# Eight instead of nine seven-product pairs in the first half of the down projection, and a later last up group

## The chip, the cores and the metric

The kernel runs on one core of a Trainium2 chip. The core has a matmul engine (PE, with its weight loads shown apart as PEld), a vector engine (DVE), a scalar engine (ACT), GpSimd (POOL) and SyncE (SP); here POOL and SP mainly issue transfers (DMAs). Each engine works through its own queue in order and waits for the others by semaphores. The metric is the device time of one execution in microseconds (us).

## The reference

One layer of a decoder: 256 tokens of width 2048, all in float32. The part that matters here is the gated MLP with a causal convolution of width 3:

```python
h = rms_norm(x, ffn_norm_g[i])
u = h @ w_up[i]                      # 2048 -> 2 x 5632
a, g = jnp.split(u, 2, axis=-1)
a = causal_dwconv(a, conv_w[i], conv_b[i])
x = x + (jax.nn.gelu(a, approximate=False) * g) @ w_down[i]   # 5632 -> 2048
gate = jax.nn.sigmoid(rms_norm(x, ple_norm_g[i]) @ w_ple_gate[i])
x = x + gate * (p[i].astype(x.dtype) @ w_ple_proj[i])
```

Before it stand the token mixers (an mLSTM and a forgetting attention) with their projections `w_in` and `w_out`.

## The kernel before, in words

**Precision.** Each float32 operand is split into a rounded part `hi` and a rest `lo`; a product is three matmuls (`hi*hi`, `hi*lo`, `lo*hi`), which accumulate in one bank of PSUM. In the down projection they stand in `product` at L1017, L1018 and L1019. The function `part` makes the split of a weight block: ACT casts `hi` (L969), then DVE subtracts to get `lo` (L970). Weights come raw from memory, 512 KB a block, by DMAs that SP issues (L955).

**Blocks and buffers.** From the up projection on, all work is a list of blocks (`Unit`), which `run_units` goes through. Blocks are split up to six ahead of the one that the matmuls are at: six sets of `hi` and `lo` (two of them under the name `w`). Raw blocks lie in six slots from the start of the down projection (three `raw`, two `w2raw`, one that shares the tag `pT`), and in three more, the two halves of `EZ` and a part of `Y`, once the last up group has no more use for these. `late["free"]`, set from `LAST_UP`, says from which block on a load may take those three.

**The order.** The Python code gives an order of importance and the dependencies. A planner then sets each engine's queue at compile time by estimated times. So a matmul of a later block may stand ahead of one of an earlier block if the plan expects that one's operands to be late; matmuls into one bank keep their order.

**The up projection.** Eleven groups of 16 blocks. After a group, ACT moves its four banks to `EZ` (`up_rows`, L869), DVE transposes into `Y` (L193), 16 small DMAs issued by POOL move the result back to `EZ` (L199), and then six steps (`up_act`) finish it: `first`, an ACT copy (L881); four convolution steps, each one ACT instruction (L886) and two of DVE (L889); and `last`, an ACT GELU (L895), a DVE multiplication (L896), an ACT cast (L137) and a DVE subtraction (L138). These steps are hooked behind the matmuls of the following blocks. Those of the last group (number 10) fall into the down projection: behind its blocks 5, 6, 6, 7, 8 and 9 (`LAST_UP`). They yield K tiles 40 to 43, which the last two pairs use.

**The down projection.** 44 K tiles of 128, taken as 22 pairs, once for the columns 0 to 1023 (the first half, `down(0, ...)`) and once for 1024 to 2047 (the second half). A plain pair is two blocks (`eight`) of four products each: 2 x 4 x 3 = 24 matmuls. A pair of the list `SEVEN` uses a scheme in the manner of Strassen and Winograd: seven products for eight, so 21 matmuls, in four blocks (`fn1` to `fn4`) of one, two, two and two products. For that it needs sums of the left side, made during the up projection and kept in device memory (`left_sums`, `sums`), which SP loads (L1048, 512 KB into one of two places `S`), and combinations of the raw weights, four DVE subtractions (L1065, L1066, L1075, L1076). Its two raw slots come free only after the fourth split. In both halves nine pairs are in seven products. The second half takes the pairs in the order 0, 1, 2, ..., 21, so that plain pairs and pairs in seven products alternate; the first half has an order of its own, `FIRST`, which begins with the plain pairs 0, 1, 3, 5 (eight blocks), then the pairs 2, 7, 4, 6, 9, 8, 11, 10, ... with 2, 4, 6, 8, 10 in seven products.

**After it.** `sums_done` and `add_rest` add the banks into `xs`; the gate and the last projection follow.

Of the kernel before, what the change touches and what calls it, by code (L numbers as in the profile page):

```python
# [16 lines left out]
S = 256  # L17
# [7 lines left out]
KF = FF // P  # L25
# [9 lines left out]
PARTS2 = 2  # L35

SEVEN = (2, 4, 6, 8, 10, 12, 14, 16, 18)
FIRST = (0, 1, 3, 5, 2, 7, 4, 6, 9, 8, 11, 10, 13, 12, 15, 14, 17, 16, 19, 18, 20, 21)
AHEAD_DMA, AHEAD_SPLIT = 3, 3
PAD = 16  # L40


LO_SHIFT = 16
FRONT = 12
LAST_UP = 9


@with_exitstack
def layer_kernel(
# [19 lines left out]
    def bank(tag, name):  # L69
        return ps.tile([P, 512], F32, tag=tag, name=name)  # L70
# [161 lines left out]
    done = [0]  # L232
# [58 lines left out]
    def wsrc(w, k0, kb, c0, n):  # L291
        return w[0, k0 * P : (k0 + kb) * P, c0 : c0 + n].rearrange("(k p) n -> p k n", p=P)
# [524 lines left out]
    with tc.tile_pool(name="ffn", bufs=1) as fp:  # L817
# [7 lines left out]
        def uT(k, n=1):  # L825

            u, k0 = ((uA, 0), (uB, KD), (uC, KD + 8))[(k >= KD) + (k >= KD + 8)]
            return u[:, k - k0 : k - k0 + n, :]
# [75 lines left out]
        late = {}  # L904
# [70 lines left out]
        def run_units(us, first_late, gate):  # L975
            loaded = split = 0
            for i, u in enumerate(us):
                if i == first_late:
                    v = apool.tile([P, 6, BLK], F32R, tag="aTa", name="w2", bufs=2)
                    room.update(late=2, pT=1, e0=1, e1=1, ring=1)  # L980
                    late.update(gate=gate, free=i + LAST_UP + 1, hi=v[:, 0:2], lo=v[:, 2:4],
                                S=v[:, 4:6].rearrange("p b (i c) -> p b i c", c=256))
# [12 lines left out]
                        break  # L995
                u.fn(*u.parts)

        def down(c0, X_tag, P_tag, sums_done, done, at, pairs):

            banks, seen, us = {}, {}, []
            plain = [p_ for p_ in pairs if p_ not in SEVEN]
            last7 = [p_ for p_ in pairs if p_ in SEVEN][-1]
            total = {"P1": len(SEVEN), "P5": len(SEVEN), "P6": len(SEVEN), "P7": len(SEVEN)}
            for t in range(NT):
                for n in range(2):
                    total[t, n] = 2 * len(plain) + (len(SEVEN) if (t, n) != (1, 1) else 0)

            def product(key, ah, al, hi, lo):  # L1010
                if key not in banks:
                    banks[key] = bank(P_tag if isinstance(key, str) else X_tag, f"dn{key}")
                    seen[key] = 0
                o = banks[key]
                first, last = seen[key] == 0, seen[key] == total[key] - 1
                seen[key] += 1
                pe.matmul(o, ah, hi, start=first, stop=False)  # L1017
                pe.matmul(o, ah, lo, start=False, stop=False)  # L1018
                pe.matmul(o, al, hi, start=False, stop=last)  # L1019

            def left(k, t):
                a = uT(k)[:, 0]
                return a[:, t * P : (t + 1) * P], a[:, 256 + t * P : 256 + (t + 1) * P]

            def half(v, n):
                return v[:, n * 512 : (n + 1) * 512]

            def eight(k, hook):
                def fn(hi, lo):
                    hi, lo = hi[:, 0], lo[:, 0]  # L1030
                    for t in range(NT):
                        for n in range(2):
                            product((t, n), *left(k, t), half(hi, n), half(lo, n))
                    if hook is not None:
                        hook(banks)
                return Unit([wsrc(w_down, k, 1, c0, 1024)], fn)

            def seven(p_, hook):
                k = 2 * p_
                st = {}  # L1040

                def S(i):
                    v = st["S"][:, i - 1]
                    return v[:, 0:P], v[:, P:256]

                def split1(hi, lo):
                    v = late["S"][:, SEVEN.index(p_) % 2]
                    nc.sync.dma_start(out=f32(v).rearrange("p i c -> p (i c)"), in_=sums[SEVEN.index(p_)])  # L1048
                    st["S"] = v
                    part(hi[:, 0:512], lo[:, 0:512], first.raws[0][:, 0:512])  # L1050

                def fn1(hi, lo):
                    product("P1", *left(k, 0), half(hi, 0), half(lo, 0))

                def split2(hi, lo):
                    part(hi, lo, first.raws[1])

                def fn2(hi, lo):
                    product((0, 0), *left(k + 1, 0), half(hi, 0), half(lo, 0))
                    product((0, 1), *S(4), half(hi, 1), half(lo, 1))  # L1060


                def split3(hi, lo):
                    ra, rb_ = first.raws
                    dve.tensor_sub(half(ra, 0), half(ra, 1), half(ra, 0))  # L1065
                    dve.tensor_sub(half(ra, 1), half(rb_, 1), half(ra, 1))  # L1066
                    part(hi, lo, ra)

                def fn3(hi, lo):
                    product("P5", *S(1), half(hi, 0), half(lo, 0))  # L1070
                    product("P7", *S(3), half(hi, 1), half(lo, 1))

                def split4(hi, lo):
                    ra, rb_ = first.raws
                    dve.tensor_sub(half(rb_, 1), half(rb_, 1), half(ra, 0))  # L1075
                    dve.tensor_sub(half(rb_, 0), half(rb_, 0), half(rb_, 1))  # L1076
                    part(hi, lo, rb_)

                def fn4(hi, lo):
                    product((1, 0), *left(k + 1, 1), half(hi, 0), half(lo, 0))  # L1080
                    product("P6", *S(2), half(hi, 1), half(lo, 1))
                    if hook is not None:
                        hook(banks)

                first = Unit([wsrc(w_down, k + i, 1, c0, 1024) for i in range(2)], fn1, split1, 0)
                first.srcs = [v.rearrange("p k n -> p (k n)").unsqueeze(1) for v in first.srcs]
                return [first, Unit([], fn2, split2, 0), Unit([], fn3, split3, 0), Unit([], fn4, split4, 2)]

            for p_ in pairs:
                if p_ in SEVEN:  # L1090
                    us.extend(seven(p_, sums_done if p_ == last7 else None))
                else:
                    for k in (2 * p_, 2 * p_ + 1):
                        us.append(eight(k, done if k == KF - 1 else at.get(k)))
            return us
# [9 lines left out]
        def sums_done(c0):  # L1105

            def f(b):
                both = xs[:, 1, c0 : c0 + 1024].rearrange("p (n c) -> p n c", n=2)
                x00, x01 = (xs[:, 0, c0 + n * 512 : c0 + (n + 1) * 512] for n in range(2))
                right = xs[:, :, c0 + 512 : c0 + 1024]  # L1110

                def twice(v):
                    return v.unsqueeze(1).broadcast_to([P, 2, 512])

                a = ring[:, 2]
                act.copy(a, b["P1"])
                dve.tensor_add(x00, b["P1"], x00)
                dve.tensor_add(a, b["P6"], a)
                dve.tensor_add(right, twice(b["P5"]), right)
                dve.tensor_add(both, twice(b["P7"]), both)  # L1120
                dve.tensor_add(x01, x01, a)
                dve.tensor_add(both, both, twice(a))
            return f

        def add_rest(c0):
            def f(b):
                for n in range(2):
                    for t in range(NT):
                        xc = xs[:, t, c0 + n * 512 : c0 + (n + 1) * 512]
                        dve.tensor_add(xc, b[t, n], xc)  # L1130
                    sumsq(ssq3, c0 // 512 + n, 512)
            return f
# [16 lines left out]
        def x3_columns(*ks):  # L1149
            return lambda *_: [column(x3s[k // 4], k % 4, get_x3T()[:, k], g_ple[:, k : k + 1]) for k in ks]  # L1150
# [116 lines left out]
        us = []  # L1267
        for q in range(KF // 4):
            us += up_group(q)
        first_late = len(us)  # L1270
        us += down(0, "aux", "mm", sums_done(0), add_rest(0), {}, FIRST)
        us += down(1024, "mm", "aux", sums_done(1024), add_rest(1024),
                   {23: x3_squares(0), 27: x3_squares(1),
                    31: x3_columns(0, 1, 2, 3), 35: x3_columns(4, 5, 6, 7)}, range(KF // 2))
        for c0, n in ((0, 512), (512, 512), (1024, 512), (1536, 512)):
            g_ = (units(token_group(w_ple_gate, all_k, get_x3T, c0, n, gate_done(c0, n), tag="aux"))
                  if c0 < D - n else last_group(c0, n))
            p_ = units(token_group(w_ple_proj, [0], lambda: pT["t"], c0, n, proj_done, tag="mm"))
# [7 lines left out]
            at = len(g_) // 2  # L1286
            us += g_[:at] + p_ + g_[at:]
        for q in range(KF // 4):
            for i, job in enumerate(up_act(q)):
                at = (8, 9, 10, 11, 12, 13) if q < KF // 4 - 1 else (5, 6, 6, 7, 8, LAST_UP)  # L1290
                with_after(us[KD * (q + 1) + at[i]], job)
        run_units(us, first_late, gate_at)

# [29 lines left out]
```

## Time and profile before

| what | value |
|---|---|
| median of three runs | 1254.69 us (1253.94 to 1255.78) |
| the profiled execution | 1255.1 us, span 1253.4 us |
| PE busy | 1243.8 us, 99% of the span, 5887 matmuls |
| DVE busy | 832.2 us, 66% |
| ACT busy | 684.9 us, 55% |
| POOL busy | 210.4 us, 17% |
| DMA traffic | 271.27 MB, 216 GB/s in the mean |

The span runs from the first to the last instruction of the program; the execution's own time has 1.7 us more around it. A busy PE is not PE at its fastest: the shown duration of a matmul (389 ns) overlaps with that of the next, so the pace is read from the distance between starts, and a granted clock below 1.00 shows as busy time too. In rows by engine the number before the bracket is busy time, and a bracket tells how long the engine was idle before the instruction and who ended it. A row `x3` has merged three instructions.

### The profile page before, as it was taken

To read this page: it belongs to the slowest core of one execution; us is meant where nothing else is said; L and a number is where in the kernel's file an instruction comes from. 1 tells how busy PE (TensorE), PEld (TensorE's weight loads), DVE (VectorE), ACT (ScalarE), POOL (GpSimd) and SP (SyncE) were. 2 spreads that over 40 slices of the span, in tenths; PEclk is the share of its full clock that TensorE was granted. 3 is DMA by queue.
4 is the path that set the end of the run, shared out by engine and by line. 5 is a ranking of instruction groups with operands and counts; after the bars stand their busy time and mean duration, and the time that the engine had idled before them with its cause. 6 is when DMAs were issued, how large, how long until landed. Compare 5 with 4: busy or idle time off the path is not lost.

```text
span 1253.4 us, 16510 instructions
## 1 busy us (share of the span) xinstructions
PE 1243.8 (99%) x5887; PEld 1051.4 (84%) x5887; DVE 832.2 (66%) x1055; ACT 684.9 (55%) x964; POOL 210.4 (17%) x395
## 2 busy tenths in 40 slices
PE   9999999999999999999999999999999999999998
PEld 7899988888888888888888888888886888888887
DVE  6455568754565655665676576667669998899553
ACT  7655555545554544655565566556546555556542
POOL 2003034100214202112202220221120000050000
PEclk9999999999999999999999999999999999999999
DMA  8667766656667767778877877887897886787560
GB/s 257 177 191 198 216 201 200 191 163 171 201 185 219 218 187 211 211 221 243 235 221 217 247 232 221 224 249 211 243 270 252 291 299 201 258 259 234 172 224 34
DMA packets 133476, 271.27 MB, mean 216 GB/s; under 512 B 14007, under 2 KB 28977, under 8 KB 133393
## 3 DMA queue, kind: packets, MB, share of 16 engines
q1 hardware_dynamic: 119936, 246.51, 65.7%
q0 software_dynamic: 13072, 23.53, 6.6%
q8 instruction: 46, 0.75, 0.2%
q14 instruction: 37, 0.30, 0.1%
q10 hardware_dynamic: 385, 0.16, 0.0%
HBM read 246.54 MB, written 6.83 MB: 202 GB/s over the span
## 4 chain that ended last, share of the span: by engine, by line
PE 95%; DMA 2%; DVE 1%; ACT 1%; issue 1%; POOL 0%; SPq 0%; DVEq 0%; ACTq 0%
PE up L1257 13%; PE up L1258 13%; PE up L1256 13%; PE tg L314 10%; PE tg L313 10%; PE tg L315 10%; PE wg L345 5%; PE wg L346 2%; DMA EZ<-Y 1%; PE dnP L1018 1%; PE dnP L1019 1%; PE dnP L1017 1%; PE dn(1, 0)_8870 L1018 1%; PE dn(0, 1)_8866 L1018 1%; PE dn(0, 1)_8866 L1017 1%; PE dn(0, 0)_8862 L1018 1%
## 5 line engine op out<-in xcount | busy, mean ns | idle before, releaser
L970 DVE TENSOR_TENSOR lo<-raw,hi 128x1024 fp32r<-128x1024 f32 (+1 forms) x219 | 264.4, 1209 | 181.9 <-ACT hi L969 181.6
L969 ACT CAST hi<-raw 128x1024 fp32r<-128x1024 f32 (+1 forms) x219 | 227.3, 1041 | 236.7 <-DMA raw<-in_w_up_dram 126.9
L284 DVE TENSOR_TENSOR lo<-raw,hi 128x1024 fp32r<-128x1024 f32 (+2 forms) x161 | 178.4, 1112 | 149.2 <-ACT hi L282 142.7
L282 ACT CAST hi<-raw 128x1024 fp32r<-128x1024 f32 (+2 forms) x161 | 153.7, 960 | 149.4 <-PE tg L315 81.6
L1258 PE MATMUL up<-hi,x2T 128*128 128x512 f32 x528 | 205.5, 389 | 0.0
L1257 PE MATMUL up<-lo,x2T 128*128 128x512 f32 x528 | 205.4, 389 | 0.0
L1256 PE MATMUL up<-hi,x2T 128*128 128x512 f32 x528 | 204.8, 389 | 0.0
L199 POOL DMA_DIRECT2D EZ<-Y x176 | 93.1, 536 | 175.8 <-DVE Y L193 143.1
L1256 PEld LDWEIGHTS up<-hi,x2T 128*128 128x128 f32 x528 | 99.1, 188 | 20.6
L1258 PEld LDWEIGHTS up<-hi,x2T 128*128 128x128 f32 x528 | 99.1, 188 | 20.5
L1257 PEld LDWEIGHTS up<-lo,x2T 128*128 128x128 f32 x528 | 99.1, 188 | 20.5
L314 PE MATMUL tg<-lo,hT 128*128 128x512 f32 (+1 forms) x288 | 102.9, 357 | 0.0
L313 PE MATMUL tg<-hi,hT 128*128 128x512 f32 (+1 forms) x288 | 101.8, 358 | 0.0
L315 PE MATMUL tg<-hi,hT 128*128 128x512 f32 (+1 forms) x288 | 101.7, 354 | 0.0
L1257 PE MATMUL up<-lo,x2Tb 128*128 128x512 f32 x176 | 68.5, 389 | 0.0
L1258 PE MATMUL up<-hi,x2Tb 128*128 128x512 f32 x176 | 68.5, 389 | 0.0
L345 PE MATMUL wg<-hT,hi 128*128 128x512 f32 x192 | 67.6, 399 | 0.0
L1256 PE MATMUL up<-hi,x2Tb 128*128 128x512 f32 x176 | 65.2, 389 | 0.0
L314 PEld LDWEIGHTS tg<-lo,hT 128*128 128x128 f32 x288 | 54.1, 188 | 5.5
L315 PEld LDWEIGHTS tg<-hi,hT 128*128 128x128 f32 x288 | 54.1, 188 | 5.5
L313 PEld LDWEIGHTS tg<-hi,hT 128*128 128x128 f32 x288 | 53.7, 188 | 5.4
L346 PE MATMUL wg<-hT,lo 128*128 128x256 f32 x192 | 52.1, 284 | 0.0
(762 smaller groups left out, 2428.1 us busy)
## 6 DMA issues: line engine op xcount, KB each, us to landing
raw<-in_w_up_dram SPq DMA_DIRECT2D x176, 512.0 KB, 4.9
raw<-in_w_in_dram SPq DMA_DIRECT2D x79, 512.0 KB, 4.1
raw<-in_w_down_dram SPq DMA_DIRECT2D x43, 512.0 KB, 6.0
raw<-in_w_in_dram SPq DMA_DIRECT2D x48, 344.0 KB, 3.6
raw<-in_w_out_dram SPq DMA_DIRECT2D x32, 512.0 KB, 4.5
EZ<-Y POOLq DMA_DIRECT2D x176, 64.0 KB, 5.6
w2raw<-in_w_down_dram SPq DMA_DIRECT2D x19, 512.0 KB, 5.7
w<-sums SPq DMA_DIRECT2D x18, 512.0 KB, 4.4
```

The source lines that it names most:

```text
L199: pool.dma_start(out=c[32 * b : 32 * b + 32, a::4], in_=y[32 * a : 32 * a + 32, :, b])
L282: act.copy(hi, raw[:, :w])
L284: dve.tensor_sub(lo, raw[:, :w], f32(hi))
L313: pe.matmul(o, ah, hi[:, i, :], start=first, stop=False)
L314: pe.matmul(o, ah, lo[:, i, :], start=False, stop=False)
L315: pe.matmul(o, al, hi[:, i, :], start=False, stop=last)
L345: pe.matmul(o, h[:, i, cols], a, start=first, stop=False)
L969: act.copy(hi, raw)
L970: dve.tensor_sub(lo, raw, f32(hi))
L1256: pe.matmul(o, ah, hi[:, n], start=k == 0, stop=False)
L1257: pe.matmul(o, ah, lo[:, n], start=False, stop=False)
L1258: pe.matmul(o, al, hi[:, n], start=False, stop=k == KD - 1)
```

## The change

Four edits go together. In the first half, pair 2 is computed as a plain pair, so eight pairs are left in seven products (`SEVEN[1:]`); `down` gets this list as an argument. The order `FIRST` becomes 0, 1, 2, 3, 5, then 4, 7, 6, 9, 8, 11, 10, ...: ten plain blocks come first, and then pairs in seven products and plain ones alternate. The place `S` is chosen by a pair's number in the half's own list. And the steps of the last up group are hooked behind blocks 6, 7, 8, 9, 10 and 11 instead of 5, 6, 6, 7, 8 and 9, with `LAST_UP` 11, which moves `late["free"]` by two blocks as well. The second half's list and order stay; the left sums of pair 2 are still made and kept, as the second half uses them.

```diff
 SEVEN = (2, 4, 6, 8, 10, 12, 14, 16, 18)
-FIRST = (0, 1, 3, 5, 2, 7, 4, 6, 9, 8, 11, 10, 13, 12, 15, 14, 17, 16, 19, 18, 20, 21)
+FIRST = (0, 1, 2, 3, 5, 4, 7, 6, 9, 8, 11, 10, 13, 12, 15, 14, 17, 16, 19, 18, 20, 21)
...
-LAST_UP = 9
+LAST_UP = 11
...
-        def down(c0, X_tag, P_tag, sums_done, done, at, pairs):
+        def down(c0, X_tag, P_tag, sums_done, done, at, pairs, sevens):
...
-            plain = [p_ for p_ in pairs if p_ not in SEVEN]
-            last7 = [p_ for p_ in pairs if p_ in SEVEN][-1]
-            total = {"P1": len(SEVEN), "P5": len(SEVEN), "P6": len(SEVEN), "P7": len(SEVEN)}
+            plain = [p_ for p_ in pairs if p_ not in sevens]
+            last7 = [p_ for p_ in pairs if p_ in sevens][-1]
+            total = dict.fromkeys(("P1", "P5", "P6", "P7"), len(sevens))
...
-                    v = late["S"][:, SEVEN.index(p_) % 2]
+                    v = late["S"][:, sevens.index(p_) % 2]
                     nc.sync.dma_start(out=f32(v).rearrange("p i c -> p (i c)"), in_=sums[SEVEN.index(p_)])
...
-        us += down(0, "aux", "mm", sums_done(0), add_rest(0), {}, FIRST)
+        us += down(0, "aux", "mm", sums_done(0), add_rest(0), {}, FIRST, SEVEN[1:])
...
-                    31: x3_columns(0, 1, 2, 3), 35: x3_columns(4, 5, 6, 7)}, range(KF // 2))
+                    31: x3_columns(0, 1, 2, 3), 35: x3_columns(4, 5, 6, 7)}, range(KF // 2), SEVEN)
...
-                at = (8, 9, 10, 11, 12, 13) if q < KF // 4 - 1 else (5, 6, 6, 7, 8, LAST_UP)
+                at = (8, 9, 10, 11, 12, 13) if q < KF // 4 - 1 else (6, 7, 8, 9, 10, LAST_UP)
```

More of the change, by code (lines that the diff above doesn't have):

```diff
@@ L996, in run_units @@
                 u.fn(*u.parts)
-        def down(c0, X_tag, P_tag, sums_done, done, at, pairs):
+        def down(c0, X_tag, P_tag, sums_done, done, at, pairs, sevens):
             banks, seen, us = {}, {}, []
-            plain = [p_ for p_ in pairs if p_ not in SEVEN]
-            last7 = [p_ for p_ in pairs if p_ in SEVEN][-1]
-            total = {"P1": len(SEVEN), "P5": len(SEVEN), "P6": len(SEVEN), "P7": len(SEVEN)}
+            plain = [p_ for p_ in pairs if p_ not in sevens]
+            last7 = [p_ for p_ in pairs if p_ in sevens][-1]
+            total = dict.fromkeys(("P1", "P5", "P6", "P7"), len(sevens))
             for t in range(NT):
                 for n in range(2):
-                    total[t, n] = 2 * len(plain) + (len(SEVEN) if (t, n) != (1, 1) else 0)
+                    total[t, n] = 2 * len(plain) + (len(sevens) if (t, n) != (1, 1) else 0)
             def product(key, ah, al, hi, lo):
@@ L1089, in down @@
             for p_ in pairs:
-                if p_ in SEVEN:
+                if p_ in sevens:
                     us.extend(seven(p_, sums_done if p_ == last7 else None))
```

## The prediction

> **What bounds the kernel.** I read the page first, then windows over the stages, the waits, and DVE and ACT around the waits. The page:
>
> ```profile
> span 1253.4 us, 16510 instructions
> PE 1243.8 (99%) x5887; PEld 1051.4 (84%) x5887; DVE 832.2 (66%) x1055; ACT 684.9 (55%) x964; POOL 210.4 (17%) x395
> ```
>
> PE bounds the whole: what is not a matmul costs only where PE stands idle or runs slowly. Where that is in the down projection, the windows show (PE, PEld, DVE, ACT and POOL busy, then the granted clock, the DMA share and GB/s):
>
> ```profile
> 914.55:946.53 31.98, 31.98 (x143) 26.41 (x141) 22.70 (x25) 18.49 (x24) 8.48 (x16) 1.00 0.90 258
> 946.53:954.84 8.31, 5.42 (x21) 3.52 (x20) 7.73 (x14) 4.86 (x6) 0.00 (x0) 1.00 0.65 233
> 954.84:958.25 3.41, 3.41 (x9) 2.64 (x8) 3.41 (x4) 1.29 (x2) 0.00 (x0) 0.50 0.98 308
> 958.25:965.00 6.75, 6.64 (x29) 5.16 (x28) 6.68 (x9) 4.43 (x5) 0.00 (x0) 1.00 0.86 305
> 965.00:1034.32 69.32, 69.32 (x305) 56.92 (x305) 66.34 (x73) 38.83 (x42) 0.00 (x0) 1.00 0.85 285
> 1034.32:1140.00 105.68, 105.68 (x468) 87.51 (x467) 94.89 (x112) 59.78 (x74) 16.89 (x32) 1.00 0.74 236
> ```
>
> PE is full everywhere but in 946.5 to 965, where it idles and then has half the clock for 3.41 us. The matmuls there (timeline of PE):
>
> ```profile
> 914.55 0.39 PE L1017 MATMUL dn(0, 0)_7999<-hi,uA 128*128 128x512 f32 x1
> ...
> 936.31 0.39 PE L1017 MATMUL dnP<-hi,uA 128*128 128x512 f32 x1
> ...
> 950.34 0.50 PE L1018 MATMUL dnP<-w 128*128 128x512 f32 x1 [1.15 <-DVE w L970]
> ...
> 952.81 0.50 PE L1017 MATMUL dn(1, 0)_8007<-hi,uA 128*128 128x512 f32 x1 [1.28 <-ACT hi L969]
> ...
> 954.28 0.50 PE L1017 MATMUL dn(0, 0)_7999<-hi,uAb 128*128 128x512 f32 x1 [0.45 <-ACT hi L969]
> ...
> 1034.32 0.39 PE L1017 MATMUL dn(0, 0)_8862<-hi,uA 128*128 128x512 f32 x1
> ```
>
> The eight plain blocks ahead of the first `dnP` are 96 matmuls in 936.31 - 914.55 = 21.76 us, so 0.2267 us each. The first half has 13 x 24 + 9 x 21 = 501 of them: 113.58 us at this pace. It took 1034.32 - 914.55 = 119.77. **The first half loses 6.19 us**, all of it between 948 and 963; the half clock is 3.41 x 0.5 = 1.7 of that. The second half, with nine pairs in seven products as well, loses nothing (105.68 busy of 105.68).
>
> Who is late? DVE, by groups, and what it did in the stretch:
>
> ```profile
> L970 DVE TENSOR_TENSOR lo<-raw,hi 128x1024 fp32r<-128x1024 f32 x14 | 16.9, 1220 | 5.4 <-ACT hi L969 5.4
> L970 DVE TENSOR_TENSOR lo<-raw,hi 128x512 fp32r<-128x512 f32 x5 | 3.4, 686 | 1.4 <-ACT hi L969 1.4
> L1076 DVE TENSOR_TENSOR w2raw<-w2raw 128x512 f32<-128x512 f32 x4 | 2.8, 689 | 0.1
> L889 DVE SCALAR_TENSOR_TENSOR Y<-Y,cT 128x254 f32<-128x254 f32 x4 | 1.8, 470 | 0.0
> L889 DVE SCALAR_TENSOR_TENSOR Y<-Y,cT 128x255 f32<-128x255 f32 x4 | 1.7, 473 | 0.0
> L896 DVE TENSOR_TENSOR Y<-Y,EZ 128x1024 f32<-128x1024 f32 x1 | 1.2, 1224 | 0.6 <-ACT Y L895 0.6
> L138 DVE TENSOR_TENSOR uC<-Y,uC 128x1024 fp32r<-128x1024 f32 x1 | 1.2, 1217 | 0.0
> ...
> 931.28 0.69 DVE L970 TENSOR_TENSOR lo<-raw,hi 128x512 fp32r<-128x512 f32 x1 [0.72 <-ACT hi L969]
> ...
> 960.80 2.35 DVE L970 TENSOR_TENSOR lo<-raw,hi 128x1024 fp32r<-128x1024 f32 x2
> ...
> 931.28:938.24 6.96, 6.96 (x32) 5.75 (x32) 5.66 (x7) 2.86 (x3) 2.66 (x5) 1.00 0.98 274
> 931.28:963.15 31.87, 28.88 (x116) 22.31 (x116) 29.16 (x38) 19.56 (x24) 2.66 (x5) 0.95 0.83 265
> ```
>
> Two subtractions in a row take 2.35 us, one 1.22, so each further one costs 1.13, and a half one about 0.60. A pair in seven products costs DVE 3 x 1.13 + 5 x 0.60 = 6.4 us and gives PE 21 x 0.2267 = 4.76 us of work: DVE falls 1.6 behind. A plain pair costs it 2.26 and gives 5.44: DVE gains 3.2. The order before puts 2, 4 and 6 in seven with only 7 between them, and into the same stretch fall the last up group's steps, 1.8 + 1.7 + 1.2 + 1.2 = 5.9 us. So DVE is busy 29.16 of 31.87 us, and is late.
>
> **Check of this reading on before.** PE without a loss would begin the second block of pair 9 (the sixth plain pair) at 914.55 + 5 x 5.44 + 3 x 4.76 + 2.72 = 958.75, and needs its `lo` one matmul later, at 958.98. DVE ends it, the second of the two at 960.80, at 963.15: 4.2 late, against the 6.19 lost. The excess of 2.0 is mainly the half clock.
>
> **The change, part by part.**
> *Pair 2 plain instead of seven:* 24 - 21 = 3 matmuls more, 3 x 0.2267 = **+0.68** on the path. It takes 6.4 - 2.26 = 4.1 us from DVE, one cast less than four on ACT, and one load of sums (512 KB) from SP; the last two lie beside PE and count nothing.
> *Order:* the first pair in seven starts on PE at 914.55 + 5 x 5.44 = 941.75 instead of 936.31, and 4 and 6 no longer touch. The check point moves to 941.75 + 4.76 + 5.44 + 4.76 + 2.72 = 959.43, `lo` at 959.66.
> *DVE up to there:* 29.16 - 4.1 = 25.1 us of work from 931.28, plus idle time. The least idle is that of before, 31.87 - 29.16 = 2.7. More comes if loads are late, since DVE now catches up with them:
>
> ```profile
> 933.50 1.05 ACT L969 CAST w<-w2raw 128x1024 fp32r<-128x1024 f32 x1 [2.25 <-DMA w2raw<-in_w_down_dram]
> ...
> 927.84 0.33 SPq L955 DMA_DIRECT2D raw<-in_w_down_dram  x1
> ...
> raw<-in_w_down_dram SPq DMA_DIRECT2D x1, 512.0 KB, 10.4
> ```
>
> The tenth load of the projection landed at 933.5 and the twelfth at 927.84 + 10.4 = 938.2 (the issue view of 927 to 929). The sizes and slots of the first twelve loads are unchanged, so I keep these times. After the change these are the last plain block and the second half of pair 4. Up to 938.24 DVE then has only 2 x 1.13 + 2 x 0.60 = 3.5 us to do in 6.96, where before it did 5.66: 2.2 us more idle, 4.9 in all. DVE therefore reaches the check point between 931.28 + 25.1 + 2.7 = 959.1 and 961.3, against 959.66: 0.6 early to 1.6 late. **Loss left:** from 0 to 1.6 plus the excess of 2.0, so 0 to 3.6. I take 1.5: the later end for DVE, as the loads' rows are of this very stretch, without a half clock, as the lateness is less than half of that before.
> *Were PE not able to go on with pair 9* while pair 6's last split is out, the bound is harsher: that split is done 2.26 earlier, at 959.0, and wanted at 951.95 + 3.40 + 0.23 = 955.6. That is 3.4, with a half clock 5.1: the upper end of my range. Before, PE did go on, with pair 9 (tiles 18 and 19, in `uB`) ahead of pair 6's last products (tile 13, in `uAb`):
>
> ```profile
> 957.42 0.63 PE L1017 MATMUL dn(1, 1)_8011<-w,uB 128*128 128x512 f32 x1
> ...
> 965.74 0.39 PE L1017 MATMUL dn(1, 0)_8007<-w,uAb 128*128 128x512 f32 x1
> ```
>
> *Steps one or two blocks later:* they issue one copy, four ACT and eight DVE instructions, GELU, multiplication, cast and subtraction; no sums (pairs 20 and 21 are plain), no DMA, nothing on SP or POOL.
>
> ```profile
> 934.51 6.41 DMA EZ<-Y
> 941.02 1.06 ACT L881 COPY Y<-EZ 128x1024 f32<-128x1024 f32 x1 [0.69 <-DMA EZ<-Y]
> 950.77 1.06 ACT L895 ACTIVATE Y<-Y 128x1024 f32<-128x1024 f32 x1 [3.45 <-DVE Y L889]
> 951.73 1.03 ACT L969 CAST hi<-w2raw 128x1024 fp32r<-128x1024 f32 x1
> ...
> 950.99 0.33 SPq L955 DMA_DIRECT2D Y<-in_w_down_dram  x1
> ```
>
> The first step waits for data that land at 940.9, now as before, behind POOL's moves, which stay. So moving it counts 0 by itself. The GELU held ACT for 3.45 us with the cast at 951.73 queued behind it, and PE waited for just such casts (1.28). With the steps spread, splits rank ahead of them; I count this nowhere, since it is the same lateness of DVE. The three late slots open two blocks later: their first load went out at 950.99, behind the steps' last readers, so the gate itself did not bind: 0.
> *The place `S` in the other order:* 0; both first places are loaded before the projection starts.
>
> **Sum:** -6.19 + 0.68 + 1.5 = -4.0 us. The profiled execution was 1255.1, so 1251.1; it lies 0.4 above the median 1254.69, so the forecast is **1250.7**. The ends: no loss left gives -5.5, 1249.2; a loss of 5.1 gives -0.4, 1254.3.
>
> **A rule of the Trainium skill.** The half clock followed gaps of 1.15, 1.28 and 0.45 us. "TensorE: Matmul & The Clock Gate", section "Why this matters for your kernels", asks for no idle gap over some 3 us and has one idle window bring the half clock back; its window of 3413 ns agrees with the 3.41 us here, its condition doesn't: no gap came near it. By the trace, several short gaps are enough.
>
> **Rivals.**
> 1. *The loss only moves:* DMA, not DVE, sets it, or the plan puts the steps' GELU ahead of pair 6's casts again. Then 3 to 6.2 us stay: -2.5 to +0.7, 1252.2 to 1255.4. For it: a DMA share of 0.98 before 938.24. Against: from 965 on, a share of 0.85 and DVE at 66.34 of 69.32 lose nothing. Chance 0.17.
> 2. *The half clock isn't due to these gaps* and stays with its 1.7 us: 1250.7 + 1.7 = 1252.4. For it: the skill's rule just told. Against: it starts directly behind the gaps, and nowhere else in the projection. Chance 0.04.
> 3. *Slower:* the loss splits in two, at the end of pair 4 (its fourth split has the twelfth load, the combinations and the steps' conversions ahead of it on DVE) and at pair 6, and each brings a half clock: 6.19 - 1.7 = 4.5 of idle time as before, plus 2 x 1.7, plus 0.68, against 6.19: +2.4, and any more idle beyond it; 1257.1 to 1258. It decides once the idle time fails to fall. For it: the twelfth load's late landing. Against: 4.1 us less work. Chance 0.09.
>
> **How the numbers follow.** The forecast has 0.70. 0.2% of this time, 2.5 us, is about what a measurement can tell from no change: rivals 1 and 2 lie within it (0.21), the forecast beyond it (0.70), rival 3 on or over it (0.09). The range goes from the loss-free 1249.2, less 0.4 for the spread of the runs, to 1254.3, which leaves out rival 3 and the end of rival 1.
>
> **What would show it.** 5890 matmuls on PE. The first `dnP` 27.2 us behind the first matmul of the projection. First half 113.58 + 0.68 + 1.5 = 115.8 us long (114.3 if loss-free). No granted clock of 0.50 in it. DVE's waits for loads between 931 and 938 grow by about 2 us. The second half unchanged at full PE. The prediction is wrong if PE waits as long around pairs 4 and 6, or a new gap appears elsewhere.

## The result and the profile after

The changed kernel takes 1252.49 us in the median (1251.05 to 1254.66, 18 runs), the kernel before 1255.91 (1252.47 to 1257.75, 18 runs, the three shown earlier among them). The ratio is 0.9977 (95% interval 0.9969 to 0.9984): faster by 2.9 us, between 2.0 and 3.9. Timed once more on another occasion it is 0.9973 (0.9963 to 0.9983). The forecast was 4.0 us, 1250.7, with a range up to 1254.3.

The page after, then the windows over the projection (PE, PEld, DVE, ACT and POOL busy, granted clock, DMA share, GB/s) and, last, over the first 20 us of the program:

```profile
span 1251.1 us, 16509 instructions
PE 1242.3 (99%) x5890; PEld 1051.7 (84%) x5890; DVE 829.6 (66%) x1049; ACT 684.1 (55%) x962; POOL 211.4 (17%) x395
```

```profile
916.27:943.47 27.20, 27.20 (x122) 22.52 (x120) 19.02 (x18) 15.26 (x17) 8.47 (x16) 1.00 0.93 289
943.47:955.90 12.43, 12.43 (x56) 10.32 (x55) 11.74 (x18) 8.40 (x11) 0.00 (x0) 1.00 0.69 246
955.90:957.45 1.55, 0.42 (x2) 0.00 (x1) 1.52 (x3) 1.10 (x2) 0.00 (x0) 1.00 0.93 336
957.45:1031.93 74.48, 74.48 (x328) 61.67 (x329) 71.28 (x77) 42.68 (x46) 0.00 (x0) 1.00 0.82 287
1031.93:1140.00 108.07, 108.07 (x478) 89.51 (x477) 99.24 (x116) 64.19 (x77) 16.90 (x32) 1.00 0.72 235
0.00:20.00 20.00, 16.62 (x81) 14.21 (x82) 10.56 (x18) 12.89 (x31) 7.13 (x23) 0.91 0.83 263
```

The timeline of PE, and DVE and ACT around the one gap that is left:

```profile
916.27 0.39 PE L1017 MATMUL dn(0, 0)_7999<-hi,uA 128*128 128x512 f32 x1
...
943.47 0.39 PE L1017 MATMUL dnP<-w,uA 128*128 128x512 f32 x1
...
957.45 0.50 PE L1017 MATMUL dn(1, 0)_8007<-hi,uAb 128*128 128x512 f32 x1 [1.13 <-ACT hi L969]
...
1031.93 0.39 PE L1017 MATMUL dn(0, 0)_8853<-hi,uA 128*128 128x512 f32 x1
```

```profile
942.39 1.05 ACT L881 COPY Y<-EZ 128x1024 f32<-128x1024 f32 x1 [1.11 <-DMA EZ<-Y]
...
954.45 1.22 DVE L138 TENSOR_TENSOR uC<-Y,uC 128x1024 fp32r<-128x1024 f32 x1
955.58 0.68 DVE L1076 TENSOR_TENSOR w2raw<-w2raw 128x512 f32<-128x512 f32 x1
...
956.35 1.04 ACT L969 CAST hi<-w2raw 128x1024 fp32r<-128x1024 f32 x1 [1.12 <-DVE w2raw L1076]
957.43 1.23 DVE L970 TENSOR_TENSOR lo<-w2raw,hi 128x1024 fp32r<-128x1024 f32 x1
```

The first half now takes 115.67 us (from 916.27 to 1031.93; here and below differences are taken before the times are rounded, so a last digit can be off by one) instead of 119.77. It holds 504 matmuls, 114.26 us, so 1.40 is lost instead of 6.19. One gap is left, before pair 6's last products. The rows show what it waited for: the cast at 956.35 waited for the combination L1076, and that stood in DVE's queue behind the steps' last subtraction (L138).

The projection starts 1.71 us later than before (916.27 against 914.55). I put this down to the program's start, long before the projection: PE had half the clock there for one stretch in this execution (0.91 over the first 20 us, which is 0.09 x 20 = 1.8 us), and 1.00 in the profile of before. So the two profiled executions differ by only 1255.1 - 1252.8 = 2.3 us, while the first half differs by 4.10.

### The profile page after: what moved, and what is told of

The parts are those of the page before. It is cut to its first block, busy times and chain, and to the rows that moved or that the text cites. A ratio compares the mean times of both kernels' runs of the same rounds, so it can differ in the third digit from the quotient of the medians.

```text
span 1251.1 us, 16509 instructions
## 1 busy us (share of the span) xinstructions
PE 1242.3 (99%) x5890; PEld 1051.7 (84%) x5890; DVE 829.6 (66%) x1049; ACT 684.1 (55%) x962; POOL 211.4 (17%) x395
## 4 chain that ended last, share of the span: by engine, by line
PE 95%; DMA 2%; DVE 1%; ACT 1%; issue 0%; POOL 0%; SPq 0%; DVEq 0%; ACTq 0%; POOLq 0%
PE up L1257 13%; PE up L1256 13%; PE up L1258 13%; PE tg L314 10%; PE tg L313 10%; PE tg L315 10%; PE wg L345 5%; PE wg L346 2%; PE dnP L1018 1%; PE dnP L1019 1%; DMA EZ<-Y 1%; PE dnP L1017 1%; PE dn(0, 1)_8857 L1018 1%; PE dn(1, 0)_8861 L1019 1%; PE dn(1, 0)_8861 L1018 1%; PE dn(0, 1)_8857 L1017 1%
## 5 line engine op out<-in xcount | busy, mean ns | idle before, releaser
L970 DVE TENSOR_TENSOR lo<-raw,hi 128x1024 fp32r<-128x1024 f32 x222 | 271.0, 1222 | 177.4 <-ACT hi L969 177.0
L969 ACT CAST hi<-raw 128x1024 fp32r<-128x1024 f32 x222 | 233.2, 1051 | 250.0 <-DMA raw<-in_w_up_dram 102.3
```

Source lines behind the costliest of these rows:

```text
L969: act.copy(hi, raw)
L970: dve.tensor_sub(lo, raw, f32(hi))
```

## The experiments

Where a time is counted "from the first matmul", it is from the first matmul of the down projection. The loss is the first half's length less its matmuls (501 or 504 of 0.2267 us). In three orders the plan mixes the end of the first half with the start of the second; there the way from the first matmul to the program's last instruction is compared, which without any loss is 113.58 + 219.1 = 332.7 us with nine pairs and 333.4 with eight (219.08 and 219.16 follow the first half before and after; in more_traffic 220.15 do, so 1.0 us of its 339.9 arose later). Each row is one profiled execution. Where a kernel was timed several times, that one can be far from its median: it was the slowest of 12 in nine_twelve_plain, the slowest of 11 in early_data_after and the fastest of 12 in early_data_before.

| kernel | copy of the first step, us from the first matmul | first half, us | loss, us | first matmul to the end, us |
|---|---|---|---|---|
| before | 26.47 | 119.77 | 6.19 | 338.8 |
| before_again | 26.14 | 119.45 | 5.87 | 338.5 |
| steps_alone | 25.97 | 119.25 | 5.67 | 338.3 |
| short_steps | 24.97 | 115.53 | 1.95 | 334.6 |
| early_data_before | 20.18 | 115.61 | 2.03 | 334.7 |
| after | 26.13 | 115.67 | 1.40 | 334.8 |
| after_again | 25.19 | 114.75 | 0.49 | 333.9 |
| order_alone | 26.76 | 116.34 | 2.08 | 335.5 |
| more_traffic | 30.22 | 119.69 | 5.43 | 339.9 |
| early_data_after | 26.19 | 117.99 | 3.73 | 337.1 |
| quarter_on_act | 24.46 | 115.90 | 1.64 | 334.7 |
| nine_ten_plain | 26.72 | mixed | 3.1 | 335.8 |
| nine_twelve_plain | 27.72 | mixed | 4.7 | 337.4 |
| eight_wider | 25.74 | mixed | 2.0 | 335.4 |

### The order without the spread steps, and the spread steps without the order

```diff
 # order_alone, against the changed kernel
-LAST_UP = 11
+LAST_UP = 9
-                at = (8, 9, 10, 11, 12, 13) if q < KF // 4 - 1 else (6, 7, 8, 9, 10, LAST_UP)
+                at = (8, 9, 10, 11, 12, 13) if q < KF // 4 - 1 else (5, 6, 6, 7, 8, LAST_UP)
 # steps_alone: the same two lines the other way round, in the kernel before
```

> The changed kernel with the last up group's steps back at blocks 5, 6, 6, 7, 8 and 9 (LAST_UP 9): only the order and the eight pairs are new. Theory D (DVE's backlog sets the loss): DVE's work is that of the changed kernel, so its first half stays at 115.7 us (114.26 of matmuls and 1.4 of loss), at most 1 us more, and no half clock. Rival S (the spreading of the steps is what helps): the first half loses 4 to 6 us again, 118 to 120 us.

> The kernel before with only the steps moved to blocks 6 to 11 (LAST_UP 11): nine pairs and the old order. Theory D: DVE has the same work in the same stretch, so the first half stays between 118.5 and 120 us (113.58 of matmuls, 5 to 6.2 of loss). Rival S: most of the gain is here, 115 to 116 us.

The order alone: 116.34 us, one gap at the same place. The steps alone: 119.25 us. So nearly all of the gain belongs to the order with its eight pairs, and the spreading by itself is worth nothing that these runs show. The row for the gap on PE in order_alone, and the window of steps_alone, which surprised: its gaps (0.66, 1.27, 0.45 and 1.16 us) are much like those of before, but its clock is 1.00.

```profile
956.23 0.50 PE L1017 MATMUL dn(1, 0)_8007<-hi,uAb 128*128 128x512 f32 x1 [1.42 <-ACT hi L969]
```

```profile
946.00:965.00 19.00, 15.25 (x62) 10.86 (x61) 18.34 (x25) 10.24 (x12) 0.00 (x0) 1.00 0.68 227
```

### Less DVE work in the steps

```diff
 # short_steps, against the kernel before
-                        dve.scalar_tensor_tensor(out=c_[:, j, d:S], in0=a_[:, j, 0 : S - d],
+                        e = S if q < KF // 4 - 1 else d + 8
+                        dve.scalar_tensor_tensor(out=c_[:, j, d:e], in0=a_[:, j, 0 : e - d],
...
-                dve.tensor_mul(by_run(c_), by_run(c_), runs(Z[:, :, 128:256]))
+                m = 4 if q < KF // 4 - 1 else 1
+                dve.tensor_mul(by_run(c_)[:, 0:m], by_run(c_)[:, 0:m], runs(Z[:, :, 128:256])[:, 0:m])
```

> The kernel before, with the DVE work of the last up group's steps cut: the eight convolution instructions work on 8 columns instead of 254 or 255, the multiplication on a quarter of its width (this leaves part of the convolution and of the gate out for K tiles 40 to 43). Theory D: DVE has some 3.5 us less to do in the stretch, so its lateness of 4.2 us falls to about 0.7 and the half clock goes with it: first half 114.2 to 115.5 us. Rival L (the weight loads set the loss): they are unchanged, first half 119 to 120 us.

The groups of DVE show what was cut, from 3.5 and 1.2 us:

```profile
L890 DVE SCALAR_TENSOR_TENSOR Y<-Y,cT 128x8 f32<-128x8 f32 x8 | 1.3, 219 | 0.0
L898 DVE TENSOR_TENSOR Y<-Y,EZ 128x256 f32<-128x256 f32 x1 | 0.4, 413 | 0.0
```

The first half takes 115.53 us, at the edge of what was expected: 3.0 us less DVE work, 3.9 us less loss than in before_again, of which 1.2 may be the earlier copy (24.97 against 26.14). The weight loads were left as they were. DVE's work behind the copy is part of what sets the loss.

### Both kernels once more

> The kernel before, profiled once more. The prediction counted the half clock behind the gaps as part of the loss of 6.19 us in every execution. The kernel with only the steps moved lost 5.67 us without any half clock, so this is in doubt. If the half clock belongs to these gaps, it is here again and the first half takes 119.8 us; if it comes only in some executions, the first half takes 118 to 118.5 us without it, and the gain of the change is 1.5 us smaller in such executions.

> The changed kernel, profiled and timed once more, to stand beside the next one. First half 115.7 us (1.4 of loss), no half clock in it, whatever the start of the program does; 2.5 to 4 us faster than the kernel before.

before_again had no half clock in the projection, with gaps much like before's, and lost 5.87 us all the same:

```profile
914.30 0.39 PE L1017 MATMUL dn(0, 0)_7999<-hi,uA 128*128 128x512 f32 x1
...
949.76 0.50 PE L1018 MATMUL dnP<-w 128*128 128x512 f32 x1 [0.84 <-DVE w L970]
...
952.24 0.50 PE L1017 MATMUL dn(1, 0)_8007<-hi,uA 128*128 128x512 f32 x1 [1.28 <-ACT hi L969]
...
959.99 0.50 PE L1017 MATMUL dnP<-hi,w 128*128 128x512 f32 x1 [1.15 <-ACT hi L969]
...
946.00:965.00 19.00, 15.06 (x61) 10.67 (x60) 18.34 (x25) 10.52 (x12) 0.00 (x0) 1.00 0.66 224
940.44 1.05 ACT L881 COPY Y<-EZ 128x1024 f32<-128x1024 f32 x1 [2.81 <-DMA EZ<-Y]
```

So the half clock, 1.7 us of slower matmuls, cost the first half 0.3 us at most between these two executions. In its place before_again has a gap at 959.99 that before lacks: while PE waits for DVE anyway, slow matmuls fill time that would be idle. after_again lost 0.49 us, 114.75 in all; in the same timing as the next kernel its ratio was 0.9973.

### Nine pairs, and wider distances

```diff
 # nine_ten_plain, nine_twelve_plain, eight_wider, against the changed kernel
-FIRST = (0, 1, 2, 3, 5, 4, 7, 6, 9, 8, 11, 10, 13, 12, 15, 14, 17, 16, 19, 18, 20, 21)
+FIRST = (0, 1, 3, 5, 7, 2, 9, 4, 11, 6, 13, 8, 15, 10, 17, 12, 19, 14, 16, 18, 20, 21)
+FIRST = (0, 1, 3, 5, 7, 9, 2, 11, 4, 13, 6, 15, 8, 10, 17, 12, 14, 19, 16, 18, 20, 21)
+FIRST = (0, 1, 2, 3, 5, 4, 7, 9, 6, 11, 8, 13, 10, 15, 12, 17, 14, 19, 16, 18, 20, 21)
...
-        us += down(0, "aux", "mm", sums_done(0), add_rest(0), {}, FIRST, SEVEN[1:])
+        us += down(0, "aux", "mm", sums_done(0), add_rest(0), {}, FIRST, SEVEN)      # the two with nine
```

> The changed kernel with nine pairs in seven products again, but ten plain blocks first and plain pairs between: order 0, 1, 3, 5, 7, 2, 9, 4, 11, 6, 13, 8, 15, 10, 17, 12, 19, 14, 16, 18, 20, 21. Theory D: in the stretch up to the third pair in seven DVE has what it has in the changed kernel, so the loss there is 1.4 us, on 113.58 of matmuls: first half 115.0 us, unless 14, 16 and 18 in a row lose something at the end. Rival (the smaller number of pairs is what helps): 118 to 120 us.

> The changed kernel with nine pairs in seven products and twelve plain blocks first: order 0, 1, 3, 5, 7, 9, 2, 11, 4, 13, 6, 15, 8, 10, 17, 12, 14, 19, 16, 18, 20, 21. Theory D: DVE has one plain pair more before the first pair in seven, 3.2 us of lead, more than the 1.4 us that the changed kernel still loses; so no loss up to pair 6, and the first half takes 113.6 to 114.3 us, 1.4 to 2.1 less than the changed kernel's. The two neighbours 8, 10 and 12, 14 and 16, 18 put DVE 1.6 us behind each, which the lead covers. Rival: neighbours in seven lose as 4 and 6 did in the kernel before, 116 us or more.

> The changed kernel with one plain pair more between the pairs 4 and 6 and the gap closed at the end: order 0, 1, 2, 3, 5, 4, 7, 9, 6, 11, 8, 13, 10, 15, 12, 17, 14, 19, 16, 18, 20, 21. The changed kernel's only gap stands before pair 6's last products; here they come 5.44 us later, while the copy starts at the same time. Theory T: no loss there, first half 114.3 us plus what the neighbours 16 and 18 lose at the end (the order with three such neighbouring pairs lost about 2 us at one of them): 114.3 to 116.3 us. Rival: the loss comes at any third pair, 115 to 116 us with the gap before pair 6 again.

(In nine_ten_plain the pairs 14, 16 and 18 stand in a row. By the code, the splits of 18 run up to six blocks ahead, so its sums go into the place of those of 14 before the last product of 14, which then uses the wrong sums. The work is the same.)

All three miss. nine_ten_plain has the gap of order_alone in its place, 1.4 us, and 0.4 more late in the half, for the sums of the three in a row. Its copy starts when order_alone's does (26.72 and 26.76), and up to 1000 us it loses as much: the distances between the starts of its matmuls add up to 2.0 us over the pace, against 2.0 in order_alone. So up to there the spacing sets the loss, and not the number of pairs, which the rival had; the rest of the 3.1, some 1.0 us, comes late, against 0.68 saved. nine_twelve_plain has only short gaps early (some 1.5 us in all by the starts), but loses 2.2 us at its neighbours 12 and 14; eight_wider has no gap up to 1010 us, which bears out the reading of the pair 6 gap, and then loses at the neighbours 16 and 18. The rows: waits of nine_ten_plain, PE of nine_twelve_plain, windows of eight_wider.

```profile
PE dn(1, 0)_8007 L1017 <- ACT hi L969: 1.4, 1, 1.4
PE dnP L1017 <- DMA w<-sums: 0.4, 1, 0.4
```

```profile
1004.60 0.50 PE L1017 MATMUL dnP<-w 128*128 128x512 f32 x1 [0.91 <-ACT w L969]
1006.11 0.50 PE L1018 MATMUL dnP<-w 128*128 128x512 f32 x1 [0.78 <-DVE w L970]
```

```profile
940.00:1010.00 70.00, 70.00 (x310) 57.97 (x310) 66.06 (x77) 42.88 (x48) 0.00 (x0) 1.00 0.81 275
1010.00:1025.00 15.00, 13.86 (x60) 10.57 (x59) 14.12 (x15) 8.46 (x10) 0.00 (x0) 1.00 0.76 252
```

So neighbours in seven can lose without any steps near them, though not each pair of them did: 8 and 10 in nine_twelve_plain show no gap. Nine pairs with thirteen plain ones cannot avoid such neighbours once ten or twelve plain blocks stand first and two plain pairs last. With eight pairs the changed kernel's order has none. That is what the 0.68 us for pair 2 buy. Timed, nine_twelve_plain has the ratio 0.9988 (0.9979 to 0.9997) and eight_wider 0.9984 (0.9975 to 0.9993): neither beats the changed kernel.

### More traffic

```diff
 # more_traffic, against the changed kernel: behind the first of the last group's sixteen moves
+    with tc.issue_after(traced()):
+        spare = kp.tile([2, P, 1024], F32, name="spare")
+        for k in range(2):
+            pool.dma_start(out=spare[k], in_=w_up[0, k * P : (k + 1) * P, 0:1024])
```

> The changed kernel with 1 MB of idle copies (two of 512 KB, device memory to device memory) issued by POOL behind the first of the last group's sixteen moves, that is around 924 us. Rival L (the weight loads of that stretch set what loss is left): at 270 to 290 GB/s this is 3.6 us of traffic, the tenth to fourteenth loads land 2 to 4 us later and the first half loses that much more, 118 to 119.5 us. Theory D with slack in the loads: under 1 us more, 115.7 to 116.7 us.

The loss is 5.43 us, as rival L said, but not for its reason. The first rows are POOL's, then ACT's copy, and DVE's wait for pair 4's second load:

```profile
921.63 0.54 POOL L879 DMA_DIRECT2D EZ<-Y  x1 [10.96 <-DVE Y L193]
922.17 1.10 POOL L884 DMA_DIRECT2D spare<-in_w_up_dram  x2
...
934.32 2.16 POOL L879 DMA_DIRECT2D EZ<-Y  x4 [2.38 <-DMA spare<-in_w_up_dram]
...
945.09 1.05 ACT L891 COPY Y<-EZ 128x1024 f32<-128x1024 f32 x1 [3.98 <-DMA EZ<-Y]
...
934.94 0.69 DVE L1076 TENSOR_TENSOR raw<-raw,raw 128x512 f32<-128x512 f32 x1 [0.98 <-DMA raw<-in_w_down_dram]
```

Pair 4's second load was there 934.94 - 914.86 = 20.1 us after the first matmul; in the changed kernel ACT's first full cast of that pair, which waited for the same load, started 936.08 - 916.27 = 19.8 after it. So that load was not late, and the three behind it landed at most 0.9 us later than in the changed kernel. The moves were late: POOL waited for the idle copies and the copy of the first step started at 30.22 instead of 26.13, 4.1 us later. The loss rose by 4.0. But this execution has a half clock in the projection, 1.7 us of slower matmuls directly behind its gaps of 1.95 and 0.74 us, and the changed kernel has none; whether the loss would be the same without it, no run shows.

```profile
958.30:961.70 3.40, 3.40 (x7) 2.44 (x8) 3.40 (x4) 2.79 (x3) 0.00 (x0) 0.51 0.88 308
```

### Earlier data for the steps

That gave a new theory (T): the landing of the moved data, at which the steps start, sets the loss. Over the seven profiles so far with the steps' full work and an order of one of the two kernels, the loss follows the copy with a slope of one. In the old order, loss = copy - 20.3 (20.28, 20.27, 20.30); in the new one, copy - 24.7 (24.73, 24.70, 24.68, 24.79). The copies lie within 0.5 us of each other in the old order and within 1.6 in the new one, but for more_traffic with its half clock. DVE shows why the copy matters. In the four of the new order its last wait before the gap is for the first result of the steps behind the copy (L886); in the three of the old order it waits, just behind the copy, for a cast that ACT does after it (and once more, 0.6 us, for the steps' GELU). In the changed kernel this wait ends at 944.11; from there to the end of the gap DVE is busy for 13.27 of 13.34 us, and in the 14.11 us ahead of it for 9.29. The row of the changed kernel, then that of more_traffic:

```profile
944.11 2.95 DVE L889 SCALAR_TENSOR_TENSOR Y<-Y,cT 128x255 f32<-128x255 f32 x7 [1.57 <-ACT Y L886]
```

```profile
946.80 2.95 DVE L899 SCALAR_TENSOR_TENSOR Y<-Y,cT 128x255 f32<-128x255 f32 x7 [4.25 <-ACT Y L896]
```

```diff
 # early_data_before and early_data_after, against the kernel before and the changed one
-            move(y, Z)
+            if last_one:                                   # group 10 alone
+                for n in range(16):
+                    i, j = n // 4, n % 4
+                    (nc.sync if n % 2 else pool).dma_start(out=Z[32 * j : 32 * j + 32, i::4],
+                                                           in_=y[32 * i : 32 * i + 32, :, j])
+            else:
+                move(y, Z)
 # quarter_on_act, against early_data_after
-                    (nc.sync if n % 2 else pool).dma_start(out=Z[32 * j : 32 * j + 32, i::4],
+                    (act if n % 4 == 3 else pool).dma_start(out=Z[32 * j : 32 * j + 32, i::4],
```

> The kernel before, with the last up group's sixteen moves issued by POOL and SP in turn instead of by POOL alone; order, pairs and steps as before. In the runs so far the loss of the first half follows, microsecond for microsecond, the time at which the first step's copy starts on ACT (counted from the first matmul of the projection): 26.47, 26.14 and 25.97 us with 6.19, 5.87 and 5.67 of loss in the old order; 30.23, 26.77, 26.12 and 25.19 us with 5.43, 2.08, 1.40 and 0.49 in the new one. Theory T (the landing of the moved data sets the loss; splits queue behind the steps): the copy starts 3 to 5 us earlier and the loss falls by as much, first half 114.5 to 116.5 us. Theory D in its plain form (the sum of DVE's work sets it): it falls by 1 us at most, 118.4 to 119.8 us.

> The changed kernel with the same edit of the moves. Theory T: the copy starts 3 to 5 us earlier, no loss is left, first half 114.3 to 114.6 us, and the time is 0.2 to 1.2 us below the changed kernel's. Against it: SP issues eight more transfers between its weight loads; should those come late, 1 to 3 us are lost instead.

> The changed kernel with four of the last up group's sixteen moves issued by ACT, so that SP's weight loads keep their place (with eight on SP the copy started at 25.96 us and the weight loads behind them landed late: first half 118.0). Theory T: the copy starts 1 to 3 us earlier than the 25.2 to 26.1 us of the changed kernel, nothing is lost, first half 114.3 to 114.6 us. Rival: the copy stays where the plan puts it among the casts, 25 us or later, and the first half stays at 114.7 to 116 us.

early_data_before bears out T: the copy comes 6.0 us earlier than in before_again and the loss falls from 5.87 to 2.03, in the old order and with nine pairs. Rows of ACT and PE:

```profile
934.87 1.04 ACT L887 COPY Y<-EZ 128x1024 f32<-128x1024 f32 x1
...
950.14 0.50 PE L1023 MATMUL dn(1, 0)_8007<-hi,uA 128*128 128x512 f32 x1 [0.83 <-ACT hi L975]
```

It does not fall all the way to zero, which the line would have. From 936.90 to its last gap at 957.50 DVE is busy for 20.47 of 20.60 us, so no wait is left there that earlier data could shorten: DVE's work itself binds, which is near to theory D.

```profile
936.90:957.50 20.60, 19.56 (x85) 15.42 (x83) 20.47 (x28) 13.05 (x17) 0.00 (x0) 1.00 0.85 308
```

early_data_after missed: SP's weight loads stood behind the moves (below: the first after them at 933.69), the plan put the copy behind casts at 26.19 (the expectation of quarter_on_act has 25.96 for it, counted from the second matmul), and PE waited for DVE (1.81). A half clock directly behind that gap adds 0.09 x 19 = 1.7 us (the window is in the last section); the gap and the slow matmuls make up nearly all of the loss of 3.73. quarter_on_act left SP alone; its copy came at 24.46, with ACT idle ahead of it for a weight load's landing (0.79), and the loss was 1.64, off the line. Here the weight loads do bind: pair 4's first load was cast 935.00 - 915.29 = 19.7 us after the first matmul, against 934.14 - 916.27 = 17.9 in the changed kernel, DVE waited 2.08 us for that cast, and from then on to 957.13 it was busy for 21.16 of 21.48 us. SP and PE of early_data_after, ACT and DVE of quarter_on_act:

```profile
926.61 6.98 SPq L879 DMA_DIRECT2D EZ<-Y  x3
933.69 1.08 SPq L961 DMA_DIRECT2D raw<-in_w_down_dram  x2
...
948.75 0.50 PE L1024 MATMUL dn(1, 0)_8007<-lo,uA 128*128 128x512 f32 x1 [1.81 <-DVE lo L976]
```

```profile
939.75 1.05 ACT L887 COPY Y<-EZ 128x1024 f32<-128x1024 f32 x1 [0.79 <-DMA w2raw<-in_w_down_dram]
...
935.65 0.69 DVE L976 TENSOR_TENSOR w<-raw,w 128x512 fp32r<-128x512 f32 x1 [2.08 <-ACT w L975]
```

Timed, the ratios are 0.9994 (0.9984 to 1.0003) for early_data_before, 0.9986 (0.9977 to 0.9996) for early_data_after and 0.9985 (0.9976 to 0.9994) for quarter_on_act. The first of these is less than its profile promises; its executions lie between 1251.1 and 1256.9, and the profiled one is the fastest, so it isn't typical of them, and why they spread so is open. That of early_data_after is its slowest, so its 3.73 us need not be typical either.

## Why the prediction was right

**The loss in the old order** (6.19 us, DVE late at the pairs in seven with the steps between): right in its place and its engines; before_again, steps_alone and short_steps agree.

**Pair 2 plain, +0.68, and the order:** right. 504 matmuls and a first `dnP` at 27.20 us, both as said; order_alone keeps all but 0.7 of the gain, which its later copy (26.76 against 26.13) accounts for.

**Loss left, 1.5:** 1.40 and 0.49 in two profiles. The first half was forecast at 115.8 us and took 115.67 and 114.75; no half clock in it, as said. DVE late at a pair in seven is the right mechanism, but the agreement of 1.5 and 1.40 is in part luck. I worked it out for the second block of pair 9, where PE didn't wait at all. The loss arose before pair 6's last products, the place of the harsher bound of 3.4, which I took for the upper end of the range alone. Pair 6's last split was done 957.43 + 1.23 - 916.27 = 42.4 us after the first matmul, not 959.0 - 914.55 = 44.5: that DVE came 2 us earlier than that bound had it makes up for the place.

**The steps' move, 0:** right.

**Three terms of the working were wrong, and their errors did not show in the sum.** First, "the excess of 2.0 is mainly the half clock": without a half clock the loss is 5.87, so in this order the half clock added about nothing. The excess lies in late products and casts, but at which of them it arises was not worked out. Second, "I keep these times" for the loads: the tenth load of the projection was there at 931.14 - 916.27 = 14.9 us after the first matmul instead of 933.50 - 914.55 = 19.0, and the twelfth at 19.8 instead of 23.7, so DVE idled less than I feared, 6.95 - 5.24 = 1.7 us in the stretch for which I gave 3.5:

```profile
931.14 1.05 ACT L969 CAST w<-raw 128x1024 fp32r<-128x1024 f32 x1 [1.38 <-DMA raw<-in_w_down_dram]
936.08 2.02 ACT L969 CAST hi<-raw 128x1024 fp32r<-128x1024 f32 x2 [1.31 <-DMA raw<-in_w_down_dram]
...
933.00:939.95 6.95, 6.95 (x32) 5.74 (x32) 5.24 (x8) 2.65 (x3) 2.79 (x6) 1.00 1.03 312
```

Third, I took the landing of the moved data for a fixed point without a price, and summed up DVE's work over the whole stretch. In the two kernels and their nearest relatives the runs show a chain instead: the moves land, the copy starts, and what DVE and ACT have in their queues from there on comes late by as much. Work ahead of the copy has slack, work behind it has none. With the data earlier the chain no longer sets the loss: in early_data_before DVE's own work does, in quarter_on_act a weight load. The change helps because it takes a pair in seven out of the part behind the copy and sets the deadlines later: by the two lines, an estimate, 24.7 - 20.3 = 4.4 us more room for the copy. Less the 0.68 for pair 2 this is 3.7 us at the same landing, and 4.1 in the first pair of profiles, where the copy also came 0.3 earlier.

**The rivals:** the loss did not move on (1), the half clock did not stay in the projection (2), and no gap came at pair 4's end (3).

**Forecast 4.0, measured 2.9 and 3.4:** the first half gave 4.1 in the one pair of profiles and 4.7 in the other, both more than the timed difference. Both profiles of the changed kernel have the half clock at the program's start and begin the projection about 2 us later; neither of before has. Of the 14 profiles five have it (short_steps, early_data_after and nine_twelve_plain too) and begin the projection at 915.95 to 916.73; the other nine begin it at 914.00 to 915.30. In these five PE's longest wait for the first input is 1.7 to 2.6 us, in the other nine at most 1.5; this stands ahead of everything that the change touches. Whether the changed program meets it more often or this was chance was not settled: the granted clock was below 1.000 in 19 of the 25 timed executions of the changed kernel and in 31 of 63 of before (8 of 19, 14 of 23 and 9 of 21 on three occasions), where the gaps of the projection can lower it as well. The forecast time, 1250.7, lies 1.8 below the measured 1252.49; 1.2 of that is the median of before, 1255.91 over 18 runs against the 1254.69 of the three that I started from.

## What to carry to other kernels

When late steps of one stage are hooked into the next, look for the moment at which their data land and count only the work behind it: that work, not the engine's sum over the stage, sets who is late, as long as the engine has idle time ahead of it. Spacing out the blocks that cost the side engines more than they give the matmul engine can be worth more than the saving of one such block. And slow matmuls in a stretch that waits anyway need not add to the loss (between before and before_again they added 0.3 us at most), while in early_data_after nothing that the run shows hid them: take the clock's cost from a second execution, not from the clock.

## What was not expected of the hardware

The half clock did not go by one rule of the gaps. It came behind gaps of 1.15, 1.28 and 0.45 us in the kernel before, behind 1.95 and 0.74 in more_traffic and behind a single one of 1.81 in early_data_after (0.91 over the stretch below); it did not come behind 0.84, 1.28, 0.45 and 1.15 us in before_again, nor behind 0.66, 1.27, 0.45 and 1.16 in steps_alone. So the prediction's "several short gaps are enough" does not hold of every execution.

```profile
946.00:965.00 19.00, 17.19 (x69) 13.73 (x68) 18.85 (x23) 11.07 (x13) 0.00 (x0) 0.91 0.86 276
```

The Trainium skill, "TensorE: Matmul & The Clock Gate", section "Why this matters for your kernels", asks for gaps under some 3 us; here shorter ones were followed by a half clock in three of these five executions, while the single gaps of 1.13 to 1.43 us in the changed kernel, order_alone and nine_ten_plain were not. A further surprise was how near the slope between copy and loss is to one: 1.6 us of loss for 1.6 of delay between after_again and order_alone, and 4.0 for 4.1 in more_traffic, where a half clock is part of it.
